# Solving the 16x16 triangular blocks of an RWKV-7 layer on GpSimd instead of VectorE, in outer-product form

## The chip, the cores and the metric

One core of a Trainium2 chip runs the whole kernel in float32. The metric is device time in microseconds. Engines are named as in the profile: PE (TensorE matmuls; PEld its weight loads), DVE (VectorE), ACT (ScalarE), POOL (GpSimd) and SP (SyncE, which issues all the DMAs of this kernel).

## The reference

One layer of a hybrid decoder, 1024 tokens by 1024 channels:

```
u = rmsnorm(h);  proj = u @ w_in          # q k v | r k v | decay, aaa, gate loras | branch gates A, B
y_attn = sliding_window_attention(q, k, v) @ w_branch_attn     # window 128, 8 heads, sinks
y_rwkv = rwkv7_time_mix(r, k, v, w, a, g) @ w_branch_rwkv      # 8 heads of 64
h = h + (sigmoid(gate_a)*y_attn + sigmoid(gate_b)*y_rwkv) @ w_out
h = h + square(relu(rmsnorm(h) @ w_ff_in)) @ w_ff_out
```

The time mix is a recurrence over tokens with a 64x64 state S per head:

```
sa = S a_t;   S = S * w_t + sa b_t^T + v_t k_t^T;   y_t = S r_t
```

## The kernel before

**Phase 1** makes the projections of u, the attention and the recurrence. The recurrence works on 8 units: 4 pairs of heads by 2 halves of the sequence, 512 tokens each, in chunks of 64 tokens. In a chunk the sequential rule becomes a triangular system, and its inverse X = (I - L)^-1 (64x64, unit triangular) is needed for every chunk and head, 16 of them in a unit.

A unit has three parts. `unit_e` prepares: it shifts and scales r, k, v, the decays and the loras, multiplies them on PE, and masks the products into SA (which holds L) and SR. It then takes the 16x16 diagonal blocks of L out of SA, through DRAM (`ln_d`, eight small DMAs at L549, two back at L551), into the tile LT: one partition for each of 128 groups of 8 columns of a block. In LT, NL (16 by 16) is the block, XL (8 by 16) the part of the inverse that this partition solves, loaded with rows of the identity (L542), and XM (8 by 16) a scratch. A memset on POOL (L552) puts ones on the diagonal of NL. The forward substitution is a loop of 15 steps on DVE: step t multiplies the solved entries 0..t-1, and the identity's entry at t, with column t of NL (L573), and sums the products into entry t of XL (L574). The result goes to DRAM (`lx_d`, L575).

`unit_m` brings XL back into XT by eight DMAs (L597), into a tile that POOL has cleared (L591), transposes it on DVE (XD, L599) and builds the 64x64 inverses from the 16x16 ones by small matmuls (ps_z, ps_x). `unit_c` is the recurrence proper: for each of 8 chunks ry (L644), G (L646), pu, UV (L651), pd, sbd (L664), one after the other between PE and DVE; then py, a group norm and the store.

**The order.** Python traces `unit_m(n)`, `estage(n+1)` (which is `unit_e`), `unit_c(n)`, and then a list of fills: projections, attention blocks and gates named by `PLAN`. A list scheduler fixes the order of each engine's queue when the kernel is built, by priorities (the recurrence's parts stand 3000 ahead of the fills: `HP_E`, `HP_C`) and by estimated durations; on the chip each queue runs strictly in its order. SP's queue has the DMAs of the recurrence and the loads of the fills' weights (L155) in one line. Most buffers that bind units are single or double (LT, BK and G0 one, XT, AR, UV, SA two), so unit n+2 waits for unit n to be done. DVE also splits each fill's weight into two float32r parts (wlo, L157), which the fill's matmuls (ps_m, L164) wait for.

POOL has little to do in phase 1: memsets of Wp (L494), z (L414), XT (L591), Yt (L642) and LT (L552).

**After phase 1** come the rest of the gates, the branch projections, the output projection and the MLP (16 steps of seven products of a fast matrix multiplication, L996), where POOL adds weights (L967 to L989).

Of the kernel before, what the change touches and what calls it, by code (L numbers as in the profile page):

```python
# [15 lines left out]
ALU = mybir.AluOpType  # L16
AX = mybir.AxisListType
# [3 lines left out]
P = 128  # L21
# [38 lines left out]
def hybrid_block(ctx, tc, x_ap, xt_ap, win_ap, lora_ap, wbr_ap, wout_ap, wff1_ap, wff2_ap, cst_ap,  # L60
                 vec_ap, eye_ap, amk_ap, out_ap, dbg=None):
    nc = tc.nc
    V, A, G, PE = nc.vector, nc.scalar, nc.gpsimd, nc.tensor
# [185 lines left out]
    def phase1():  # L249
# [215 lines left out]
        def e4(t):  # L465
            return t.rearrange("p (a b c) -> p a b c", b=2, c=64)

        def unit_e(p, hf, lw, X):
# [50 lines left out]
            m = ep.tile([P, HALF], F32, tag="cum", name="m", bufs=1)  # L519
# [4 lines left out]
            for par in range(2):  # L524
                V.scalar_tensor_tensor(out=BK[:, :, 3 * par, :], in0=e4(kkn)[:, :, par, :], scalar=-0.5,
                                       in1=e4(Wi)[:, :, par, :], op0=ALU.mult, op1=ALU.mult)
            ARf = AR.rearrange("p a (b s) c -> p a b (s c)", s=2)
            BKf = BK.rearrange("p a (b s) c -> p a b (s c)", s=2)
            for par in range(2):
# [3 lines left out]
                for h in range(2):  # L533
                    for i, dst in enumerate((SA, SR)):
                        slot = (par + i) % 2
                        V.tensor_mul(out=dst[:, par, h::2, :], in0=pss[h][:, :, slot, :],
                                     in1=mk[:, i].unsqueeze(1).broadcast_to([P, 4, 64]))
            LT = rp.tile([P, 512], F32, tag="LT", name="LT", bufs=1)
            NL = LT[:, 0:256].rearrange("p (a b) -> p a b", b=16)
            XL = LT[:, 256:384].rearrange("p (a b) -> p a b", b=16)  # L540
            XM = LT[:, 384:512].rearrange("p (a b) -> p a b", b=16)
# [7 lines left out]
                    nc.sync.dma_start(out=lnv[q, b], in_=SA[s0:s0 + 16, q // 2, :, o:o + 16])  # L549
            for u in range(2):  # L550
                nc.sync.dma_start(out=LT[u::2, 0:256], in_=ln_d[un])  # L551
            G.memset(LT[:, 0:256:17], 1.0)  # L552
            for q in range(2):
                c0 = q * 4
                pt = pp.tile([P, 4, 128], F32, tag="s", name="pt")
# [11 lines left out]
                PE.transpose(pt[:, i], v[:, i * 128:(i + 1) * 128], ident)  # L567
            A.copy(out=UV[64:128, 0::2, :], in_=pt[0:64])
            A.copy(out=UV[0:64, 1::2, :], in_=pt[64:128])
            for t in range(1, 16):  # L570
                n = min(t, 8)
                row = NL[:, 0:t + 1, t].unsqueeze(1).broadcast_to([P, n, t + 1])
                V.tensor_mul(out=XM[:, 0:n, 0:t + 1], in0=XL[:, 0:n, 0:t + 1], in1=row)  # L573
                V.tensor_reduce(out=XL[:, 0:n, t], in_=XM[:, 0:n, 0:t + 1], axis=AX.X, op=ALU.add)  # L574
            nc.sync.dma_start(out=lx_d[un], in_=LT[:, 256:384])  # L575
            X.update(AR=AR, ARf=ARf, UV=UV, BKt=BKt, SA=SA, SR=SR, bv=bv, wc=wc, un=un)

# [121 lines left out]
        def estage(n):  # L699
            p, hf = n // 2, n % 2  # L700
            with tc.high_priority(offset=HP_E):
                if hf == 0:
                    lw = wpool.tile([P, 128], F32, tag="wraw", name="lw", bufs=2)
                    nc.sync.dma_start(out=lw, in_=lora_ap[:, p])
                    lws[p] = [ep.tile([P, 128], F32R, tag=t, name=t) for t in ("lwh", "lwl")]
                    A.copy(out=lws[p][0], in_=lw)
                    V.tensor_sub(out=lws[p][1], in0=lw, in1=lws[p][0].bitcast(F32))
                unit_e(p, hf, lws[p], xs[n])
# [56 lines left out]
    for k in range(8):  # L765
        t = bp.tile([P, T], F32, tag="yt", name="yt", bufs=3)
# [121 lines left out]
    op = ost.enter_context(tc.tile_pool(name="opool", bufs=1))  # L888
# [322 lines left out]
```

## Time and profile before

| | us |
|---|---|
| median of 3 runs (lowest to highest) | 1527.97 (1526.92 to 1528.69) |
| profiled execution, its own time | 1529.62 |
| span of its profile, first to last instruction | 1527.8 |
| PE busy (share) | 1491.3 (98%) |
| DVE busy | 1044.1 (68%) |
| ACT busy | 639.1 (42%) |
| POOL busy | 192.2 (13%) |

The span runs from the first to the last instruction; the execution's own time has 1.8 us more around it. A busy engine is not one at its peak: matmuls overlap, and their ends are modelled. Idle time of an engine that nobody waits for costs nothing. "Waits" tells for how long an engine stood still and which instruction ended it; "the chain of waits" follows the last instruction back through what released each step, and gives shares of the stretch by engine and line.

### The profile page before, as it was taken

What the parts mean: (1) busy time and instruction counts of PE and PEld (TensorE: products, weight loads), DVE (VectorE), ACT (ScalarE), POOL (GpSimd) and SP (SyncE); (2) the same over time, 40 slices, a digit from 0 to 9 for tenths busy, and PEclk for the clock granted to TensorE, in tenths of its full rate; (3) what the DMA queues carried; (4) which work ended last, traced back from release to release, by engine and by line L of the source; (5) the groups of instructions that cost most, each with busy time, mean ns of one, the idle gap of its engine ahead of it and who ended that gap; (6) DMA issues with size and microseconds to landing.
All of it is one profiled execution on the core that took longest, in us unless ns stands there. A gap on an engine that the chain in (4) does not pass through costs nothing.

```text
span 1527.8 us, 22206 instructions
## 1 busy us (share of the span) xinstructions
PE 1491.3 (98%) x8396; PEld 1177.2 (77%) x8396; DVE 1044.1 (68%) x2056; ACT 639.1 (42%) x1126; POOL 192.2 (13%) x116
## 2 busy tenths in 40 slices
PE   5999999999999999999999999999999999999998
PEld 5878777777777777788888787878787878787776
DVE  4232678888988875353656579595858687776867
ACT  6332436456545665441224354332424333423332
POOL 1000000000000000000000111323223232323230
PEclk9999999999999999999999999999999999999999
DMA  5455334334222323383433111111120111111112
GB/s 192 165 149 146 109 103 149 103 104 120 88 90 66 103 84 124 117 295 113 136 125 146 42 42 56 56 42 69 42 69 28 69 42 65 46 56 42 56 55 111
DMA packets 99771, 145.65 MB, mean 95 GB/s; under 512 B 26448, under 2 KB 48848, under 8 KB 99664
## 3 DMA queue, kind: packets, MB, share of 16 engines
q1 hardware_dynamic: 99664, 144.23, 28.8%
q8 instruction: 66, 1.08, 0.3%
q14 instruction: 41, 0.34, 0.1%
HBM read 108.54 MB, written 35.65 MB: 94 GB/s over the span
## 4 chain that ended last, share of the span: by engine, by line
PE 75%; DVE 19%; ACT 3%; issue 2%; DMA 1%; SPq 0%; DVEq 0%; ACTq 0%
PE ps_m L164 32%; PE psy L996 15%; PE psx L996 12%; DVE wlo L937 4%; DVE c L1021 2%; DVE c L1001 2%; DVE tlo L1032 2%; PE po L164 2%; PE ps_o L927 1%; PE pu L170 1%; DVE h L1094 1%; ACT c L1004 1%; ACT whi L936 1%; PE pk L246 1%; PE ps_s L170 1%
## 5 line engine op out<-in xcount | busy, mean ns | idle before, releaser
L164 PE MATMUL ps_m<-uh,wlo 128*128 128x512 f32 x576 | 235.5, 409 | 0.0
L164 PE MATMUL ps_m<-ul,whi 128*128 128x512 f32 x576 | 234.3, 407 | 0.0
L164 PE MATMUL ps_m<-uh,whi 128*128 128x512 f32 x576 | 233.0, 404 | 0.0
L996 PE MATMUL psy<-T,whi 128*128 128x512 f32 x512 | 159.6, 393 | 0.0
L164 PEld LDWEIGHTS ps_m<-uh,whi 128*128 128x128 f32 x576 | 108.6, 189 | 21.2 <-issue 0.8
L164 PEld LDWEIGHTS ps_m<-uh,wlo 128*128 128x128 f32 x576 | 108.6, 189 | 21.1 <-issue 0.6
L164 PEld LDWEIGHTS ps_m<-ul,whi 128*128 128x128 f32 x576 | 108.7, 189 | 20.2 <-issue 0.7
L996 PEld LDWEIGHTS psy<-T,whi 128*128 128x128 f32 x512 | 96.1, 188 | 21.9
L157 DVE TENSOR_TENSOR wlo<-wraw,whi 128x512 fp32r<-128x512 f32 x101 | 67.9, 687 | 56.6 <-ACT whi L156 56.4
L996 PE MATMUL psx<-tlo,whi 128*128 128x512 f32 x256 | 101.9, 398 | 4.5 <-DVE tlo L1032 4.5
L937 DVE TENSOR_TENSOR wlo<-fraw_a,whi 128x1024 fp32r<-128x1024 f32 x47 | 66.0, 1405 | 57.5 <-ACT whi L936 57.5
L936 ACT CAST whi<-fraw_a 128x1024 fp32r<-128x1024 f32 x47 | 49.3, 1049 | 129.1 <-PE psy L996 85.7
L996 PE MATMUL psx<-thi,wlo 128*128 128x512 f32 x256 | 101.6, 398 | 1.5 <-DVE h L1094 0.9
L996 PE MATMUL psx<-thi,whi 128*128 128x512 f32 x256 | 101.0, 395 | 0.0
L996 PE MATMUL psy<-T,wlo 128*128 128x512 f32 x256 | 100.6, 393 | 0.0
L967 POOL TENSOR_TENSOR fraw_a<-fraw_a,fraw_a 128x1024 f32<-128x1024 f32 x16 | 45.5, 2846 | 346.7 <-DVE s L942 345.5
L1094 DVE TENSOR_TENSOR h<-h,psx 128x1024 f32<-128x1024 f32 (+1 forms) x66 | 76.8, 1179 | 9.6 <-PE psx L996 9.6
L996 PE MATMUL psy<-tlo,whi 128*128 128x512 f32 x192 | 77.2, 402 | 3.1 <-DVE tlo L1032 3.1
L156 ACT CAST whi<-wraw 128x512 fp32r<-128x512 f32 x105 | 61.0, 619 | 45.4 <-PE ps_m L164 45.3
L996 PE MATMUL psy<-thi,wlo 128*128 128x512 f32 x192 | 75.8, 395 | 0.0
L996 PE MATMUL psy<-thi,whi 128*128 128x512 f32 x192 | 75.8, 395 | 0.0
L996 PE MATMUL psy<-B,whi 128*128 128x512 f32 x240 | 74.8, 393 | 0.0
(298 smaller groups left out, 3227.1 us busy)
## 6 DMA issues: line engine op xcount, KB each, us to landing
wraw<-win SPq DMA_DIRECT2D x72, 256.0 KB, 3.3
fraw_a<-wff SPq DMA_DIRECT2D x32, 512.0 KB, 3.2
wraw<-wff SPq DMA_DIRECT2D x32, 512.0 KB, 3.2
gate_d<-gt SPq DMA_DIRECT2D x32, 256.0 KB, 2.0
z_d<-zt SPq DMA_DIRECT2D x24, 256.0 KB, 2.3
xt<-x SPq DMA_DIRECT2D x8, 512.0 KB, 5.7
la<-wa_d SPq DMA_DIRECT2D x8, 512.0 KB, 4.3
aq<-q_d SPq DMA_DIRECT2D x8, 512.0 KB, 4.2
```

Of the source, the lines that this page charges most:

```text
L156: A.copy(out=hi[:, ks], in_=raw[:, ks])
L157: (eng or V).tensor_sub(out=lo[:, ks], in0=raw[:, ks], in1=hi[:, ks].bitcast(F32))
L164: PE.matmul(out=out, lhsT=a, rhs=b, start=(n == 0), stop=(n == last))
L170: after = PE.matmul(out=out, lhsT=lhsT, rhs=rhs, start=start, stop=stop).ins
L936: A.copy(out=hi, in_=src)
L937: V.tensor_sub(out=lo, in0=src, in1=hi.bitcast(F32))
L967: G.tensor_sub(out=a21, in0=a11, in1=a21)
L996: PE.matmul(out=out, lhsT=a, rhs=b, start=start and n == 0, stop=n == last, skip_group_check=True)
L1001: V.scalar_tensor_tensor(out=c, in0=c, scalar=0.0, in1=r2[:, (lo_, hi_)[hf]].unsqueeze(1).broadcast_to([P, 2, HALF]), op0=ALU.max, op1=ALU ...
L1021: V.tensor_sub(out=C[out], in0=C[a], in1=C[out])
L1032: V.tensor_sub(out=lo, in0=src, in1=hi.bitcast(F32))
L1094: V.tensor_add(out=ht, in0=ht, in1=ps[:, c0 % 2:c0 % 2 + step])
```

## The change

The loop of 15 steps goes to POOL and is turned round. Step t takes entry t, which is final by then, multiplies it with row t of NL from t+1 on, into XM, and adds the products to entries t+1 to 15 of XL. No entry of the diagonal is read, so the memset of ones goes. The rows solved grow from 1 to 8 as before (n). There are 15 multiplies and 15 adds in each of 8 units, where there were 15 multiplies and 15 reductions.

```
-            G.memset(LT[:, 0:256:17], 1.0)
...
-            for t in range(1, 16):
-                n = min(t, 8)
-                row = NL[:, 0:t + 1, t].unsqueeze(1).broadcast_to([P, n, t + 1])
-                V.tensor_mul(out=XM[:, 0:n, 0:t + 1], in0=XL[:, 0:n, 0:t + 1], in1=row)
-                V.tensor_reduce(out=XL[:, 0:n, t], in_=XM[:, 0:n, 0:t + 1], axis=AX.X, op=ALU.add)
+            for t in range(15):
+                n, m = min(t + 1, 8), 15 - t
+                G.tensor_mul(out=XM[:, 0:n, t + 1:], in0=XL[:, 0:n, t:t + 1].broadcast_to([P, n, m]),
+                             in1=NL[:, t, t + 1:].unsqueeze(1).broadcast_to([P, n, m]))
+                G.tensor_add(out=XL[:, 0:n, t + 1:], in0=XL[:, 0:n, t + 1:], in1=XM[:, 0:n, t + 1:])
```

## Rows read from the trace of the kernel before

**Rows 1.** The page: busy time, share of the span and instructions of each engine.

```profile
PE 1491.3 (98%) x8396; PEld 1177.2 (77%) x8396; DVE 1044.1 (68%) x2056; ACT 639.1 (42%) x1126; POOL 192.2 (13%) x116
```

**Rows 2.** Two stretches: length, busy us by engine (instructions), granted clock, DMA.

```profile
185.00:545.00 360.00, 355.38 (x3198) 266.90 (x3197) 309.50 (x1097) 201.82 (x488) 6.44 (x31) 1.00 0.33 101
640.00:860.00 220.00, 220.00 (x958) 179.09 (x957) 113.12 (x162) 65.65 (x108) 4.34 (x2) 1.00 0.45 154
```

**Rows 3.** The chain of waits, 185 to 545 us, shares by engine and line.

```profile
by line: PE ps_m L164 29.4%; PE pu L170 4.9%; PE ps_s L170 4.1%; PE po L164 3.9%; PE ry L644 3.4%; DVE LT L573 3.4%; PE pd L654 3.2%; PE ps_l L170 2.5%; PE ps_x L608 2.5%; PE ps_z L603 2.4%; DVE LT L574 2.3%; PE pt L557 2.0%; issue 1.8%; PE
```

**Rows 4.** Waits of PE's weight loads for DVE, 185 to 545: total, times, longest.

```profile
PEld pu L170 <- DVE G L646: 10.4, 27, 0.7
...
PEld ps_l L170 <- DVE k L422: 0.2, 1, 0.2
```

**Rows 5.** Groups of DVE, 185 to 545: busy us, mean ns, idle before.

```profile
L573 DVE TENSOR_TENSOR LT<-LT 128x2 f32<-128x2 f32 (+14 forms) x120 | 32.1, 267 | 3.6 <-POOL LT L552 2.0
L574 DVE TENSOR_REDUCE LT<-LT 128x1 f32<-128x2 f32 (+14 forms) x120 | 26.0, 217 | 1.5
```

**Rows 6.** Groups of POOL over the span, by shape.

```profile
L157 POOL TENSOR_TENSOR wlo<-wraw,whi 128x512 fp32r<-128x512 f32 x4 | 5.0, 1264 | 13.8 <-ACT whi L156 13.8
L591 POOL MEMSET XT<- 128x512 f32 x8 | 4.2, 526 | 118.8 <-PE pu L170 42.9 <-DMA XT<-lx_d 29.1 <-DMA LT<-eye 28.9
L414 POOL MEMSET z<- 128x1 f32 x14 | 1.4, 99 | 153.5 <-DVE r L422 84.2 <-DVE lt L422 31.5 <-DVE v L422 20.7
L552 POOL MEMSET LT<- 128x16 f32 x8 | 1.2, 154 | 69.1 <-DMA LT<-ln_d 49.0 <-DVE DZ L615 20.1
```

**Rows 7.** Waits of POOL, 185 to 545 us.

```profile
POOL LT L552 <- DMA LT<-ln_d: 47.2, 6, 19.9
```

**Rows 8.** Timeline of POOL, third unit: start, us, instruction, idle before.

```profile
286.84 0.13 POOL L552 MEMSET LT<- 128x16 f32 x1 [4.27 <-DMA LT<-ln_d]
303.09 0.12 POOL L494 MEMSET Wp<- 128x8 f32 x1 [11.07 <-DVE AR L517]
```

**Rows 9.** Timelines of POOL and DVE in the MLP.

```profile
958.47 2.41 POOL L989 TENSOR_TENSOR wa<-fraw_a,wraw 128x1024 f32<-128x1024 f32 x1 [27.18 <-DMA wraw<-wff]
960.95 3.27 POOL L967 TENSOR_TENSOR fraw_a<-fraw_a,fraw_a 128x1024 f32<-128x1024 f32 x1
959.45 2.51 DVE L937 TENSOR_TENSOR wlo<-fraw_a,whi 128x1024 fp32r<-128x1024 f32 x1
961.88 1.21 DVE L1094 TENSOR_TENSOR h<-h,psx 128x1024 f32<-128x1024 f32 x1
```

**Rows 10.** Timeline of DVE, third unit's substitution.

```profile
302.26 0.68 DVE L517 TENSOR_TENSOR AR<-kkn,Wp 128x512 f32<-128x512 f32 x1
...
307.66 0.75 DVE L422 SCALAR_TENSOR_TENSOR v<-z,vec,v 128x512 f32<-128x512 f32 x1
```

**Rows 11.** Timelines of SP, PE and DVE around three hand-overs.

```profile
238.33 0.32 SPq L575 DMA_DIRECT2D lx_d<-LT  x1
247.47 0.45 PE L170 MATMUL py<-UV,SR 128*64 128x64 f32 x8
250.50 0.70 DVE L599 STREAM_TRANSPOSE XD<-XT 128x512 f32<-128x512 f32 x1
287.93 0.14 DVE L573 TENSOR_TENSOR LT<-LT 128x2 f32<-128x2 f32 x1
305.85 0.33 SPq L575 DMA_DIRECT2D lx_d<-LT  x1
313.76 0.70 DVE L599 STREAM_TRANSPOSE XD<-XT 128x512 f32<-128x512 f32 x1
469.86 0.15 DVE L573 TENSOR_TENSOR LT<-LT 128x2 f32<-128x2 f32 x1
492.79 0.32 SPq L575 DMA_DIRECT2D lx_d<-LT  x1
```

**Rows 12.** Groups of PE, 640 to 860 us.

```profile
L164 PE MATMUL ps_m<-uh,wlo 128*128 128x512 f32 x93 | 36.8, 396 | 0.0
```

## The prediction

> **What bounds the kernel now.** I read the page's busy shares first: TensorE (PE) is busy 98% of the span, VectorE (DVE) 68%, GpSimd (POOL) 13% [rows 1]. So nearly everything off PE is beside PE's work, and the question is which of PE's small stops the change touches. The table by stretches places it: all 240 instructions that go stand between 185 and 545 us, the recurrent part of phase 1. There PE is busy 355.4 of 360 us and DVE 309.5 (86%); POOL does 6.4 us. From 640 us on, PE is dense: 958 matmuls in 220 us, 0.230 us each; the granted clock is 1.00, 2.4 GHz, in either stretch [rows 2]. The chain of waits over the 360 us shows what DVE's substitution holds: 3.4% and 2.3%, together 5.7% or 20.5 us [rows 3]. The waits of PE's weight loads show what it costs in small: 31 groups name DVE as releaser, from 10.4 us down to 0.2, and sum to 28.4 us in 82 waits [rows 4]. The reader is to see a kernel that is bound by PE, in which a busy DVE delays PE by tenths of a microsecond at a time.
>
> **The change part by part.** *What goes.* 120 multiplies (32.1 us) and 120 reductions (26.0 us) leave DVE [rows 5], 58.1 us of its 309.5, or 18.8%. The POOL memset of the diagonal goes too: 8 times 0.15 us, 1.2 us [rows 6], hidden anyway, on an engine that idles 98% of the stretch. Its cover matters in another way: it already made POOL's queue stand at the head until the DMA of LT landed, 47.2 us in 6 waits [rows 7]. The new first multiply stands there in its place, so no new kind of blocking comes to that queue; what is added is the time the 30 instructions hold it.
>
> *What DVE's relief is worth.* A wait of PE on DVE is DVE's own latency or its queue. I let the 28.4 us shrink with DVE's load: 18.8% of 28.4 is 5.3 us. The bounds: zero, as PE's fills (ps_m, the projections and gates) stand beside nearly all of it and PE's own idle time here is only 360 - 355.4 = 4.6 us; and 20.5 us, if all that the chain shows of it goes and nothing is late behind it. I take 5.3, because in [rows 4] the releaser is a DVE instruction in its queue and not the substitution alone. What is late next is DVE still, with 251 us left, and PE's own small matmuls.
>
> *What a substitution costs on POOL.* Each of the 8 units gets 15 multiplies and 15 adds. Multiply t works on min(t+1,8) rows of 15-t elements; summed over t that is 596 elements, twice 1,192. POOL's two-input instructions are seen at 512 elements (1264 ns) and 1024 (2.41 us where nothing holds it) [rows 6, 9]. That is a slope of 2.24 ns an element and 0.12 us fixed, and between two that follow each other a gap of 0.07 us (960.88 to 960.95 [rows 9]), 0.2 us fixed in all. Low: 1,192 x 2.24 ns + 30 x 0.20 us = 8.7 us. No row shows so small a two-input instruction on POOL, nor one with rows of 16 in steps. The nearest for steps is a memset: 16 elements 17 apart take 154 ns in the mean against 100 ns for one, and 512 in a row take 526 [rows 6], so some 3.6 ns an element against 0.83. The same factor 4.3 on 2.24 ns would be 9.6 ns, and 1,192 x 9.6 ns + 6 us = 17.5 us. The new instructions write in rows of up to 15 neighbours, so I stay near the low end: 11 us undisturbed.
>
> *Who disturbs it.* At 959.45 a DVE subtraction of two SBUF operands takes 2.51 us, and ends about 1.08 us after the POOL instruction that had begun at 958.47; the next on POOL then takes 3.27 instead of 2.41, and ends 2.26 us after DVE's. A DVE add of the same shape with one operand in PSUM, right after and beside POOL, takes 1.21 us [rows 9]. So those with two SBUF operands and POOL's take turns. In a substitution's stretch DVE has about ten such of 0.68 us (from AR at 302.26 to v at 307.66 seven stand in a row of this kind, two of them in [rows 10]), a third of 20 us. A POOL instruction that meets one waits half of it: 30 x 1/3 x 0.34 = 3.4 us. I take 11 + 3.4 = 14 us a substitution. Upper end: every POOL instruction behind one whole DVE instruction, 17.5 + 30 x 0.68 = 38 us. In the other direction ten DVE instructions a unit wait half a POOL instruction of some 0.3 us, with chance 11/14: 1.2 us, 9 us over 8 units; DVE's relief is then 49 us, not 58, and 5.3 becomes 4.5.
>
> The Trainium skill, "SBUF — State Buffer", section "SBUF: two separate sides", calls that pair of ports an exclusive lock: a VectorE instruction with two SBUF inputs and a GpSimd one that reads SBUF never run together, whichever starts second blocks fully. By that rule, the trace agrees: 2.51 against 1.21 us and 3.27 against 2.41; it is a rule that speaks against this move, and by it the sum is 4.5 where without it 5.3 stands.
>
> *Where 14 us stand.* Today a substitution takes 17.9 us (the third unit, 287.93 to 305.85) or 22.9 (the seventh, 469.86 to 492.79) [rows 11], some 20 between them, for DVE weaves other work in. After it come lx_d, then eight DMAs into XT, then the block transpose XD on DVE. In the even units that follows at once, 305.85 to 313.76, which is the time of two DMA trips: the substitution is the last thing late. In the odd ones (238.33 to 250.50) the end of the unit before, whose last small matmuls (py) run to 247.9, is late too, so 4 of 8 have slack of some 4 us [rows 11]. With 14 us XT is ready some 6 us earlier in four places. That moves PE's order of fills and recurrence, but adds nothing to PE's work, and gates are left over for PE after phase 1: 93 matmuls of each of three kinds on uh stand after 640 us [rows 12], 279 x 0.23 = 64 us. So I cost the shorter chain at nothing beyond the 5.3.
>
> *What is queued behind.* lx_d on SP now waits for POOL instead of DVE; behind it are the DMAs into XT and the loads of weights. On POOL the small memsets of Wp, z, XT and Yt stand behind up to 14 us of work. The memset of Wp of the next unit comes 16 us after the one that goes (286.84 to 303.09 [rows 8]), past the 14; where the two stand closer it comes up to some 2 us later, in front of an exponential on ScalarE. I cost these at 0 to 2 us and take 0.
>
> *Sum.* The profiled execution is 1529.62 us, its span 1527.8 and 1.8 around it. 1529.6 - 4.5 to 5.3, say 5, is 1524.6; it lies 1.65 us above the median 1527.97, so against the median 1523.
>
> **The rivals.** *First, no change.* PE is busy 98% of the stretch, and its fills cover DVE's substitution, so the 28.4 us are latency of the hop and not queue; the order is also laid anew. For it: PE's idle time is 4.6 us in all. Against: DVE is saturated where substitution and the next unit's preparation meet (around 302 to 308 us, one after another [rows 10]). Time: 1526 to 1530, 1528.
>
> *Second, slower: POOL comes late.* The order of every queue is fixed at build time from estimated durations. Where the estimate of POOL is shorter than the truth, XD stands at the head of DVE's queue before XT has landed, DVE stops, no weight is split (wlo), and PE stops at its next fill or at ps_z. Place: the four even units, where nothing else is late. It decides from about 20 us a substitution, 0.67 us an instruction, in today's order, and earlier where the new order counts on less. Price: with 17.5 us of work and 3.4 of turns it is 21, so 7 us later than the 14 that I count on, at four places 28 us if PE sees all of it; fills that are ready take up about half, which leaves 14 us slower, and with the 1 us or so that DVE's relief still gives there 13: 1541. At the upper end (38 us) it would be 4 x 18 = 72 and 1600, which I hold for unlikely. For it: no row shows such an instruction. Against: POOL has nothing else to do there, and its own rows are regular.
>
> *Third, much faster.* All 20.5 us of the chain go: 1507.5. For it: in the even units the substitution is the last thing late, DVE is full. Against: the paths beside it are PE's own, with gaps under a microsecond.
>
> **How the numbers follow.** My forecast, 3 to 14 us faster, has 0.36; the third rival 0.06; no change 0.28; slower 0.30. A measurement of this kernel tells 0.2%, about 3 us, from no change. So faster 0.42, same 0.28, slower 0.30. The predicted time is 1523. The forecast's own range is 1514 to 1525. For 8 in 10 the range goes from 1511 to 1542: below it lies the third rival's end, above it the upper half of the second.
>
> **What would show it.** Right: no instruction of LT on DVE, DVE busy near 251 us in what answers to the 360; POOL's 30 per unit in 10 to 17 us; lx_d issued 10 to 17 us after LT has landed, where it is about 19 to 24 today; the waits of PE's loads on DVE down by some 5 us. Wrong: POOL's substitutions over 20 us, waits of DVE at XD of microseconds, PE idle in front of ps_z or ps_m; or PE's waits on DVE unchanged although DVE has 58 us less to do.

## The result and the profile after

The changed kernel takes 1569.13 us (median; 1567.13 to 1569.49), against 1527.63 us for the kernel before in the same session: ratio 1.0268, interval 1.0255 to 1.0281, so 41.5 us slower. Its profile has a span of 1567.5 us, 39.7 more than before. First the page's busy shares, then two stretches of the span in the columns of [rows 2]; the second is moved by the 40 us, so that it holds the same work.

```profile
PE 1512.0 (96%) x8396; PEld 1192.6 (76%) x8396; DVE 1012.1 (65%) x1816; ACT 638.5 (41%) x1126; POOL 270.2 (17%) x348
```

```profile
185.00:545.00 360.00, 336.57 (x2914) 250.81 (x2912) 262.02 (x808) 183.66 (x444) 82.97 (x257) 0.95 0.30 93
...
680.00:900.00 220.00, 220.00 (x955) 179.04 (x954) 110.91 (x159) 64.30 (x106) 4.50 (x2) 1.00 0.42 145
```

From 680 us on the kernel runs as the one before: the same 220.00 us of PE busy, 955 matmuls against 958 [rows 2]. The loss lies in phase 1: PE stands for 23.4 of the 360 us, where it stood for 4.6, has done 2,914 matmuls instead of 3,198, and its granted clock is 0.95 instead of 1.00. What PE waited for, 185 to 590 us (total, times, longest), and where DVE stood in front of XD:

```profile
PE ps_z L602 <- DVE XD L598: 12.4, 2, 6.5
PE ry L643 <- DVE sbd L663: 3.2, 4, 2.0
PE ry L643 <- ACT lt L446: 2.2, 1, 2.2
```

```profile
DVE XD L598 <- DMA XT<-lx_d: 10.3, 3, 6.0
...
DVE XD L598 <- DMA LT<-eye: 2.1, 2, 1.1
```

The larger of the two stops at ps_z, in the third unit (start, duration, instruction, idle before):

```profile
311.27 0.27 POOL L573 TENSOR_TENSOR LT<-LT 128x8 f32<-128x8 f32 x1
...
311.57 0.33 SPq L574 DMA_DIRECT2D lx_d<-LT  x1
313.12 3.63 SPq L596 DMA_DIRECT2D XT<-lx_d  x8
318.12 0.71 DVE L598 STREAM_TRANSPOSE XD<-XT 128x512 f32<-128x512 f32 x1 [5.99 <-DMA XT<-lx_d]
318.88 0.18 PEld L602 LDWEIGHTS ps_z<-XD,SA 64*64 64x64 f32 x2 [6.68 <-DVE XD L598]
318.88 0.37 PE L602 MATMUL ps_z<-XD,SA 64*64 64x64 f32 x2 [6.49 <-DVE XD L598]
```

POOL ends its last add at 311.54, the result goes out at once, XT is back at 317.9. From about 312 us both DVE and PE stand at the heads of their queues, at XD and at ps_z; behind them are the masks of the next unit (DVE), its ps_s and the fills' ps_m (PE). In the kernel before the same XD found XT landed [rows 11]. Around this stop the granted clock falls (columns as in [rows 2]; the clock is the third number from the end):

```profile
312.00:319.00 7.00, 0.51 (x8) 0.32 (x7) 1.01 (x3) 0.00 (x0) 0.00 (x0) 0.65 0.38 101
319.00:327.00 8.00, 8.00 (x79) 6.23 (x81) 4.05 (x9) 0.72 (x1) 0.10 (x1) 0.50 0.44 140
```

After a stretch in which PE worked 0.5 of 7 us, it runs for 8 us at 0.50, that is 1.2 instead of 2.4 GHz, and does 79 matmuls there. In all 44.4 us of phase 1 are at 0.50; before, none were.

To sum it up I took every matmul from 150 us to the first branch projection (4,274 of them). The time from its start to the next one's start, less PE's idle time, is compared with the lower quartile of its kind in the kernel before; what lies above that I call the excess. PE's idle time rose from 6.6 to 26.3 us, the excess while the clock was at 0.50 from 0 to 22.7, and all other excess fell from 116.5 to 113.8. That is +19.7, +22.7 and -2.7, together 39.7 of the 40.1 us by which that projection comes later (745.6 against 705.5). Only the idle time is sharp: with other groupings into kinds the second term comes out at 19 to 26 us and the third at -4 to -6. The third has the sign of a relief of DVE, and two larger terms stand against it.

POOL itself kept its part. Groups of POOL in phase 1 (busy us, mean ns of one, idle before):

```profile
L573 POOL TENSOR_TENSOR LT<-LT 128x48 f32<-128x48 f32 (+13 forms) x120 | 43.4, 362 | 9.4
L571 POOL TENSOR_TENSOR LT<-LT 128x48 f32<-128x48 f32 (+13 forms) x120 | 36.2, 302 | 89.3 <-DMA LT<-ln_d 80.5
```

A substitution takes 10.3 to 14.7 us from its first to its last instruction, 12.2 in the mean of eight, where DVE's took 15.4 to 22.9, 19.7 in the mean. It is faster than the one it replaces and faster than the 14 us that I predicted, yet the kernel is slower.

### The profile page after: what moved, and what is told of

It reads as the page before. It is cut to its first block, busy times and chain, and to the rows that moved or that the text cites. A ratio compares the mean times of both kernels' runs of the same rounds, so it can differ in the third digit from the quotient of the medians.

```text
span 1567.5 us, 22196 instructions
## 1 busy us (share of the span) xinstructions
PE 1512.0 (96%) x8396; PEld 1192.6 (76%) x8396; DVE 1012.1 (65%) x1816; ACT 638.5 (41%) x1126; POOL 270.2 (17%) x348
## 3 DMA queue, kind: packets, MB, share of 16 engines
q1 hardware_dynamic: 99664, 144.23, 27.8%
## 4 chain that ended last, share of the span: by engine, by line
PE 71%; DVE 15%; DMA 4%; POOL 3%; ACT 3%; issue 3%; SPq 1%; DVEq 0%; POOLq 0%; ACTq 0%
PE ps_m L164 30%; PE psy L995 14%; PE psx L995 11%; DVE wlo L936 4%; DVE c L1020 2%; POOL LT L573 2%; DVE c L1000 2%; DVE tlo L1031 2%; POOL LT L571 2%; PE ps_o L926 1%; DVE h L1093 1%; PE po L164 1%; PE ps_s L170 1%; PE pu L170 1%; ACT c L1003 1%
```

## The experiments

Theories. **T1**: the loss lies in the order. With the loop on POOL, all five queues were laid anew, for an XT that comes earlier than POOL and the transfers can bring it; DVE stands at XD, and PE behind it. This is the second rival. **T2**: DVE and POOL hold each other up. **T3**: the new form is at fault, on whichever engine. **T4**: the fall of the clock is a loss of its own, which can be won back alone. **T5**: any order laid anew loses some 10 to 15 us by chance.

### The form, the engine, the turn-taking

```
outer_dve   -  G.tensor_mul / G.tensor_add  (new loop)       +  V.tensor_mul / V.tensor_add
odd_pool    +  if un % 2 == 1: new loop on G    else: memset of the diagonal, old loop on V
dup         old loop on V, and beside it the new loop on G, on a scratch tile (XL2, XM2)
m_low       -  with tc.high_priority(offset=HP_C):  unit_m   +  offset=0
```

> The new form of the loop with both of its instructions on DVE instead of POOL, the diagonal folded away as in the changed kernel. T1 (PE's fixed order counts on XT before POOL and the transfers deliver it, PE stands at ps_z of units 0 and 2, and its granted clock falls there) and T2 (POOL and DVE take turns and DVE's work is stretched): the form itself costs DVE about what the old one did, so about 1528, from 1520 to 1540, with no stop of PE over 3 us at ps_z. T3 (the form is at fault, whichever engine runs it): 1555 to 1575, PE standing 5 us or more at ps_z in units 0 and 2 as in the changed kernel.

Measured: 1533.56 us, ratio 1.0031 (1.0019 to 1.0043), no wait of DVE at XD for a transfer. T3 falls. The form costs DVE 46.9 us of busy time (23.3 and 23.6), the old one 58.1 [rows 5]; that the run is still 0.3% slower is a first sign that a new order has a price.

> The kernel before with the old loop on DVE, and beside it the new loop on POOL on a scratch tile whose result nobody reads: the turn-taking without the dependency. T1: up to 5 us slower than before, 1525 to 1535, though XT's transfers may queue behind nothing new. T2: the turn-taking alone costs 15 us or more, 1543 or above, DVE's remaining instructions stretched by some 25 us in all.

Measured: 1531.58 us, ratio 1.0019 (1.0009 to 1.0028). This kernel has the queues of before, instruction by instruction, and POOL's whole loop beside them. The turn-taking of the two engines costs 2.6 us, not 41. T2 falls.

> The new loop on POOL in units 1, 3, 5, 7 alone; units 0, 2, 4, 6 have the old loop on DVE. T1: the two stops of PE at ps_z (units 0 and 2) and the low clock behind them go, 1520 to 1535, PE's granted clock 1.0 up to 545 us. T2: half of the turn-taking stays, so half of the loss, 1543 to 1553.

Measured: 1557.57 us, ratio 1.0187 (1.0171 to 1.0203). Neither number: T2 had 1543 to 1553, and T1 in the narrow form that I gave it (two stops at ps_z) had this at least 22 us faster. PE does not stand at ps_z for more than 0.6 us here. The timeline of 343 to 353 us shows where it stands instead:

```profile
343.86 0.45 PE L652 MATMUL ry<-sbd,AR 128*128 128x128 f32 x2
344.39 4.92 SPq L605 DMA_DIRECT2D XT<-lx_d  x8
350.95 0.71 DVE L607 STREAM_TRANSPOSE XD<-XT 128x512 f32<-128x512 f32 x1 [7.05 <-DMA LT<-eye]
351.69 0.29 DVE L654 TENSOR_TENSOR G<-G,ry 64x128 f32<-64x128 f32 x1
...
352.04 0.69 PE L170 MATMUL pu<-G,XT 64*64 64x64 f32 x4 [7.03 <-DVE G L654]
```

XD of the fourth unit is ahead of G of the third unit's recurrence in DVE's queue. Its XT lands 7 us later than DVE gets there (the releaser is named after an older transfer of the same queue); ry is long done, G has to wait, and pu and all of PE with it. So the place is not ps_z in the even units; it is XD in DVE's queue, and whatever stands behind it.

> The changed kernel with the solver's second half (unit_m: ps_g, the XT transfers, ps_z, ps_x) put in order without its priority, so that ps_z stands on PE behind all of the next unit's ps_s; POOL's loop is untouched. T1: PE no longer stands at ps_z of units 0 and 2, the clock stays at 1.0 there, and 15 to 35 us of the 41 come back: 1530 to 1555; ps_z being later, the state chain may start later and eat part of it. T2: 1565 or above, as the turn-taking is unchanged.

Measured: 1565.33 us, ratio 1.0236 (1.0219 to 1.0253). A miss of T1's number, though its sign came: PE no longer stands at ps_z. T2's number (1565 or above) is met, but dup has already shown what the turn-taking costs. The rows give another reason: the order was laid anew again, and DVE stands at XD for longer, not shorter, five times:

```profile
DVE XD L599 <- DMA XT<-lx_d: 14.9, 4, 5.1
DVE XD L599 <- DMA wraw<-win: 4.1, 1, 4.1
```

An edit that lets the order be laid anew can't tell the order from the rest. The next kernels fix it.

### The order, held fixed

Each engine's instructions are chained in the order of another kernel by edges that hold the order of issue alone; the loop's own instructions are left free. In short:

```
+ for a, b in zip(queue, queue[1:]):                  # each engine's queue, as the other kernel has it
+     tc.add_manual_dep(b, a.name, DependencyInfo(DependencyClass.NoSync, DependencyReason.DATA), ...)
pool_old_order   the changed kernel, queues of the kernel before
none_old_order   the same, loop left out
dve_new_order    the kernel before, queues of the changed kernel
```

> The changed kernel, its loop on POOL, with every other instruction of all five engines queued in the order that it has in the kernel before (order edges alone, no waits added). T1 (the loss comes from the order that was laid anew for the POOL loop, which counts on XT earlier than it comes: DVE stands at XD, and PE behind it): the whole loss of 41 us goes and the relief of DVE shows, 1520 to 1528; DVE's substitution gone, PE's idle between 150 us and the first y matmul back from 26 to under 8 us, granted clock 1.0 throughout. T2 (turn-taking of DVE and POOL, some 26 us of stretched DVE work): the order doesn't matter, 1550 or more.

Measured: 1524.29 us, ratio 0.9980 (0.9969 to 0.9990): the whole loss is gone, and it is the fastest of the kernels that keep the whole loop. Seven of the twelve executions have a mean granted clock of 1.000 and take 1521.9 to 1524.9 us; five have 0.996 or 0.997 and take 1527.6 to 1529.4. The profiled one is among the five, and its clock was at 0.50 for 10.2 us from 322.6 us on. The medians of the seven and the five lie 5.3 us apart, and 10.2 us at half the clock are 5.1 us of lost work. T1's clock of 1.0 throughout holds for the seven alone.

```profile
185.00:545.00 360.00, 356.69 (x3192) 271.10 (x3194) 275.26 (x856) 201.35 (x487) 84.92 (x261) 0.99 0.34 101
```

> As the run with the order of before, with the loop left out on any engine (the inverses are wrong): what the relief of DVE can give at most in that order. My prediction's step says 5.3 us (18.8% of the 28.4 us that PE waits for DVE): 1523. No relief at all, because PE is the bound: 1528. If the 20.5 us of the chain were to go: 1508.

Measured: 1523.20 us, ratio 0.9974 (0.9962 to 0.9986). The relief of DVE gives some 5 us in this order, and POOL's loop takes some 1 us of it back, which is not clear of noise: the two intervals overlap. The time goes with the granted clock here too: eight executions with 0.999 or 1.000 take up to 1525.0 us, four with 0.996 or 0.997 take 1528.2 or more.

```profile
185.00:545.00 360.00, 356.51 (x3213) 270.67 (x3211) 275.89 (x869) 201.71 (x487) 5.32 (x24) 1.00 0.34 102
```

> The reverse: the old loop on DVE, all else queued in the order of the changed kernel. No POOL work at all is added. T1 (order): as slow as the changed kernel or slower, 1565 to 1600, since DVE's loop of some 20 us ends later than POOL's 12 and PE stands at ps_z for longer. T2 (POOL's turn-taking): 1525 to 1540.

Measured: 1631.30 us, ratio 1.0664 (1.0648 to 1.0679), worse than the upper end of T1. With no loop on POOL at all, the changed kernel's order is slower still, since DVE's loop needs 11.9 to 20.2 us there and ends later than POOL's. Waits of DVE and of PE:

```profile
DVE XD L600 <- DMA XT<-lx_d: 28.0, 5, 6.9
...
DVE XD L600 <- DMA LT<-eye: 14.0, 2, 7.0
```

```profile
PE ry L645 <- DVE sbd L665: 22.0, 7, 8.9
PE pd L655 <- DVE UV L652: 17.3, 3, 8.9
PE ps_z L604 <- DVE XD L600: 13.7, 2, 7.2
PE pu L170 <- DVE G L647: 9.8, 9, 7.8
```

Seven of the eight units stand at XD, and four kinds of PE's matmuls wait behind. The two runs together show the cause: the order, whichever engine solves the blocks.

### The clock

```
warm_new_order   queues of the changed kernel; in units 0 and 2, ahead of ps_z:
+ for _ in range(8): PE.matmul(out=ps[:, 0:384], lhsT=ident, rhs=LT[:, 0:384], start=True, stop=True)
```

> The changed kernel in its own order, with 8 matmuls of 128x384 on LT, whose result nobody reads, in front of ps_z of units 0 and 2, where PE otherwise stands for 5.9 and 6.5 us. T1 with the clock as a separate half (T4): ps_z starts within 1 us of where it did, the granted clock stays 1.0 at 201 and 314 us, and about 10 of the 22.7 us of matmuls at half clock come back: 1555 to 1563. If the low clock costs nothing of its own (PE waits for the chain anyway): 1567 to 1573.

Measured: 1576.64 us, ratio 1.0318 (1.0303 to 1.0333): slower than either expectation. The stops at ps_z are down to 0.81 and 1.90 us and the clock stays at 1.00 there (first row), but it falls from 233 us on instead, for 13.7 us (second row; PE busy 10.80 of 15 us, with one stop of 4.8 us at ry, 2.2 us in the changed kernel). In all 37.5 us are at 0.50 instead of 44.4. The excess at that clock is down by 4 to 5 us and PE's idle time by 7.5, not counting the stops behind the added matmuls; these 16, with those stops, take 13.5.

```profile
197.00:206.00 9.00, 8.20 (x56) 5.41 (x58) 3.54 (x9) 0.92 (x2) 0.86 (x3) 1.00 0.16 29
232.00:247.00 15.00, 10.80 (x36) 8.36 (x37) 8.04 (x29) 8.32 (x20) 0.10 (x1) 0.54 0.35 111
```

So this run does not decide T4: the clock was held up in one place and fell in another, and the mean granted clock of the executions (0.985 to 0.989) is that of the changed kernel (0.986 and 0.987). The executions of pool_old_order speak for its first half: with the same queues, 10.2 us at 0.50 go with 5.3 us more. Why the clock fell in five of them and not in seven is not known. That such a loss can be won back alone in the changed order is not shown.

### How late is too late

```
none_new_order     queues of the changed kernel, loop left out
half_new_order     queues of the changed kernel       -  for t in range(15):   +  for t in range(0, 15, 2):
double_old_order   queues of the kernel before; a second loop on a scratch tile, step by step between the first's
```

> The changed kernel's order on all five engines, with the loop left out on any engine (the inverses are wrong): LX goes out as soon as LT has landed, some 12 us earlier than in the changed kernel. If that order is right for a loop that is short enough (T1: the fixed order counts on XT at a time that POOL cannot keep): 1520 to 1530, no stop of PE at ps_z, no wait of DVE at XD over 1 us. If the order is bad by itself, whatever the loop takes (T5): 1545 or more.

> The changed kernel's order with only the even steps of the loop on POOL (the odd ones left out, the inverses are wrong): some 6 us a unit instead of 12. T1: between none and all of it in that order, with the stops of 5.9 and 6.5 us at ps_z gone or under 1 us: 1525 to 1550. T5 (the order is bad by itself): within 5 us of the changed kernel's 1569.

> The order of the kernel before, POOL's loop in every unit doubled by a second one on a scratch tile, step by step between the steps of the first: some 24 us a unit instead of 12. My prediction put the point from which a late POOL costs time in that order at about 20 us a substitution, and 7 us late at 28 us if PE sees all of it. T1 in that form: 4 us late in four units, half covered by fills, and twice the turn-taking (2 to 3 us): 1532 to 1548. If even 24 us is covered: 1524 to 1530.

Measured: none_new_order 1538.22 us, ratio 1.0064 (1.0049 to 1.0079); half_new_order 1540.73, 1.0077 (1.0060 to 1.0094); double_old_order 1538.28, 1.0076 (1.0047 to 1.0105), with executions from 1530 to 1551. The doubled loop takes 13.9 to 20.4 us a unit, 16.6 in the mean, not 24. The halved loop takes 5.4 to 7.6, 6.5 in the mean. So in the changed kernel's order 6.5 us of loop cost 2.5 us more than none (the intervals overlap), and 12.2 us cost 31; in the order of before, 12.4 us cost 1 us, and 16.6 cost 15. The 15 us have the second loop's turn-taking in them, and clock: the fastest execution, 1530.3 us, had a granted clock of 1.000, the slowest, 1551.2, of 0.990. Neither number of mine (T1's 1520 to 1530 for the first, 24 us for the last) was met, but the shape is T1's: an order gives a loop so much time, and past that it loses steeply. Waits of DVE at XD in double_old_order, where in pool_old_order there were none:

```profile
DVE XD L603 <- DMA XT<-lx_d: 4.5, 2, 2.8
```

The 15 us between none_new_order and none_old_order are in the order even without any loop; T5 has that much, and what in the order costs them is not known.

### Orders planned for a longer loop

```
plan_15, plan_30, plan_45    the changed kernel; its queues are those that came out when 15, 30 or 45
                             more steps stood on POOL ahead of the loop (they aren't in the kernel that runs)
```

> POOL's loop unchanged, all five queues in an order that was planned with 15 more steps of the same kind on POOL ahead of the first step (the steps themselves are not in the kernel that runs). PE's own matmuls between a unit's last ps_s and its ps_z are 24 to 32 us by the durations of before's trace, where the changed kernel has 21 to 27, the kernel before 30 to 38, and some 30 are needed. T1 (the order counts on XT too early): about half of the loss back, 1535 to 1555, PE's stops at ps_z under 4 us. T5 (orders laid anew are worse by chance, 10 to 15 us each, whatever they count on): within 8 us of 1569.

> As plan_15 with 30 more steps in the planning: 27 to 36 us of PE's matmuls between a unit's last ps_s and its ps_z, about what is needed. T1: no stop at ps_z over 2 us, 1520 to 1538. T5: 1545 or more.

> As plan_15 with 45 more steps in the planning: 31 to 42 us of PE's matmuls in that place, as many as before or more. T1: no wait of DVE at XD over 1 us and no stop of PE at ps_z; 1518 to 1535, a little over plan_30 if the solver now stands too late for the state chain. T5: 1545 or more.

Measured: 1537.75 us, ratio 1.0058 (1.0041 to 1.0075); 1535.80, 1.0047 (1.0031 to 1.0064); 1530.14, 1.0007 (0.9998 to 1.0017). The loop is the same, the time that the order gives it grows, and the run gets shorter each time (the intervals of the first two overlap). T1's times hold for all three, T5's for none; of T1's signs one failed, a wait of 5.9 us of DVE at XD in plan_45. All three are orders laid anew, so luck in the order may be in each; plan_15 and plan_30 are still 11 to 14 us behind pool_old_order, about T5's size. The table sets beside it PE's own matmuls between a unit's last ps_s and its ps_z, without the recurrence's ry, pu and pd, each at the median time to the next start in before's trace (mean of eight units). The chain from there over the blocks' transfers, the loop and XT took 30.4 and 31.0 us in the two units of the changed kernel where PE stopped (174.4 to 204.8 and 287.9 to 318.9).

```
kernel            PE's matmuls ahead of ps_z, us   DVE at XD for a transfer, us   loop, us   ratio
changed kernel    24.7                             12.4                           12.2       1.0268
plan_15           26.8                              2.3                           12         1.0058
plan_30           30.0                              1.1                           12.8       1.0047
plan_45           34.0                              5.9                           12         1.0007
pool_old_order    32.4                              0                             12.4       0.9980
odd_pool          33.2                             14.5                           12 / 21    1.0187
m_low             33.7                             19.0                           12         1.0236
none_new_order    24.7                              0                              0         1.0064
dve_new_order     24.7                             42.0                           17         1.0664
```

In the two units where PE stopped, counted alone and with all of PE's matmuls, the changed kernel has 23.0 and 24.3 us ahead of ps_z against a chain of 30.4 and 31.0, and stops for 5.9 and 6.5; plan_15 has 26.7 and 29.3, and stops for 1.6 and not at all. This helps to explain why 2 us more in the mean give back so much.

Two places count, PE's at ps_z and DVE's at XD: odd_pool and m_low have enough ahead of ps_z, and lose at XD. The waits at XD are an outcome of the run, so I set beside them what the queue alone has: DVE's own instructions between a unit's last mask (SR) and its XD, the loop left out, each at the median time to the next start in before's trace, idle time left out (mean of eight units). That is 16.6 us in the changed kernel, 17.6 in m_low, 20.3, 23.8 and 27.8 in plan_15, plan_30 and plan_45, and 26.7 in the order of before. In odd_pool it is 13.3 to 22.5 us in the units that POOL solves and 16.2 to 33.9 in the others. All kernels whose DVE stands at XD for 12 us or more are 1.9% to 6.6% slower (warm_new_order too, with 15.6 us and 3.2%), all with less are within 0.8%. plan_45 has one wait of 5.9 us that cost little; a wait isn't a loss by itself.

## Why the prediction was wrong

*Relief of DVE: right in the order of before.* In the order of before, the waits of PE's weight loads for DVE fall from 28.4 us [rows 4] to 22.9, by 5.5; I predicted 5.3. The run is 4.0 us faster, I predicted 4.5 to 5.3, and 1524.3 stands beside my 1523. That the numbers agree so well is in part luck: the load did not fall by 58.1 of 309.5 us but by 34 (309.50 to 275.26 [rows 2]; 275.89 with no loop anywhere), and 11% of 28.4 would have been 3.1. The 58.1 of [rows 5] is a sum of durations, and DVE's small instructions overlap their neighbours: without the loop's the rest of the kernel before keeps DVE busy for 274.4 us of that stretch, so the loop added 35.1. In the changed kernel itself the same waits rose, to 39.4 us; there the relief is not to be seen in them.

*A substitution on POOL: right in size.* 12.2 us in the mean against 14 (11 undisturbed and 3.4 for turns); the shortest takes 10.3.

*Turn-taking: too high on DVE's side.* I gave DVE 9 us more. The durations of DVE's instructions in phase 1 add up to 411.0 us without a loop and 414.1 with POOL's: 3.1, and 2.6 us of time in dup. The Trainium skill, "SBUF — State Buffer", section "SBUF: two separate sides", has the pair of ports as an exclusive lock. By that rule POOL's add of 128x16 at 310.29 (0.55 us, while DVE works on k, Wi and kkn out of SBUF, against 0.23 at 227.49 in the unit before) is held up, and the trace agrees; only the price is small here. The add undisturbed, then held up beside its neighbour on DVE:

```profile
227.49 0.23 POOL L573 TENSOR_TENSOR LT<-LT 128x16 f32<-128x16 f32 x1
...
310.06 0.70 DVE L522 TENSOR_TENSOR BK<-k,Wi 128x512 f32<-128x512 f32 x1
...
310.29 0.55 POOL L573 TENSOR_TENSOR LT<-LT 128x16 f32<-128x16 f32 x1
```

*The step that failed* is "so I cost the shorter chain at nothing beyond the 5.3". I worked the sum out in the order of before, and wrote of the new one only that it is laid anew. That order is a part of the change like the loop itself, and here the largest: with the same loop on POOL it makes 1569.1 us of 1524.3, so the term that I put at nothing is some 45 us. Some 15 of them are there with no loop at all (1538.2 against 1523.2), and the rest comes because the order puts ps_z after 24.7 us of PE's work instead of 32.4, and XD after 16.6 us of DVE's instead of 26.7, for a chain of 30 on PE's side.

*The second rival* had the mechanism and the rows that would show it (waits of DVE at XD of microseconds, PE idle in front of ps_z). Its place, the four even units, fits the two stops at ps_z, but in dve_new_order seven of eight units stand at XD. It failed in two sizes. Its point: "from about 20 us a substitution, in today's order, and earlier where the new order counts on less". In today's order it lies between 12.4 and 16.6 us (as far as the doubled loop, with its turn-taking, tells), in the new one between 6.5 and 12.2. I had weighed it as though POOL must be slower than DVE; it was enough that the order leaves POOL less time than it takes. Its price: 13 us; the two terms of the accounting are 19.7 us of idle PE and some 22.7 at half clock. I had no term for the clock, though PE's stops were the rival's content.

*First and third rival:* neither. PE's fills do cover the loop, in an order that gives them the place.

*Open:* why the changed order costs 15 us even with no loop; whether plan_45's last 6 us against pool_old_order are order or chance; how much of the 22.7 us would go with the clock alone; and what the scheduler's own estimate for the loop was: that it was too short is inferred from plan_15 to plan_45, not read.

## What to carry to other kernels

Where a scheduler lays the queues anew, as here, moving work to another engine can move everything else: the change is the new order plus the moved work, and the two have to be told apart. Hold the old order fixed and time the moved work in it, and time the old work in the new order; here the first was 0.2% faster and the second 6.6% slower. To predict, compare the time that the new queues leave for a chain (work ahead of its first consumer, on each in-order engine) with what the chain takes, transfers included; an engine that does the work faster, but not as fast as the order counts on, can make the kernel slower.

## What the runs showed of the hardware

In these traces dependent instructions on POOL have a gap between them, and independent ones overlap. In the changed kernel each begins some 0.08 us after the one before has ended:

```profile
221.00 0.30 POOL L573 TENSOR_TENSOR LT<-LT 128x55 f32<-128x55 f32 x1
221.38 0.30 POOL L571 TENSOR_TENSOR LT<-LT 128x60 f32<-128x60 f32 x1
```

In double_old_order, where two loops alternate, each begins before that:

```profile
202.14 0.21 POOL L575 TENSOR_TENSOR L<-L,LT 128x16 f32<-128x16 f32 x1
202.32 0.21 POOL L575 TENSOR_TENSOR LT<-LT 128x16 f32<-128x16 f32 x1
202.49 0.22 POOL L577 TENSOR_TENSOR L<-L 128x16 f32<-128x16 f32 x1
```

So 60 instructions took 16.6 us where 30 took 12.2 (means of eight units). An instruction of 128x60 takes 0.30 us, where 60 elements at my slope and fixed part of [rows 6, 9] are 0.25.

The granted clock was at 0.50 for 6.8 and 13.7 us from PE's two stops at ps_z on. It also fell at 375.5 us, for 6.8 us, right after a stretch in which PE was busy all the time, with small matmuls among its 96 (the last 0.5 us of the row are at 0.50 already):

```profile
368.00:376.00 8.00, 8.00 (x96) 5.82 (x93) 6.15 (x24) 1.19 (x3) 0.00 (x0) 0.97 0.15 39
```

So a busy PE in the profile does not by itself tell that the clock stays up. In the kernel before the granted clock is never at 0.50 between 22 us and its last microsecond.
